# Attention results turned three units later, and attention products half a unit sooner, in a two-layer decoder trunk

## The chip, the cores and the metric

The kernel runs on one core of a Trainium2 chip. Its metric is the device time of one execution in microseconds, here the median of three runs. A profile is one further execution, recorded instruction by instruction; its times are counted from the first instruction. A core has a matrix engine (TensorE, PE in the profile, with its weight loads shown as PEld), three engines for elementwise work (VectorE or DVE, ScalarE or ACT, GpSimd or POOL) and SyncE (SP), whose queue here issues most of the transfers between memory and the core.

## The reference

The trunk has two layers of 256 tokens by 1024 features. Each layer is a SwiGLU block, a mixer and another SwiGLU block, each with a residual and a layer norm. The mixer projects its input to u, v, q, k, values and two gates; branch A gates u with a causal position mixing of v; branch B is differential attention with 8 heads. Cut to what matters here:

```python
def _diff_attention(q, k, v, lam):
    ...
        s = jnp.einsum('bqhmd,bkhmd->bhmqk', q_blk, k).astype(jnp.float32) * scale
        ...
        p = jax.nn.softmax(s, axis=-1)
        a = p[:, :, 0] - lam * p[:, :, 1]
        return jnp.einsum('bhqk,bkhe->bqhe', a.astype(v.dtype), v)

def _mixer(...):
    ...
    o = _diff_attention(q, k, val, lam_full)
    o = _rmsnorm(o, diff_ln_g) * (1.0 - lam_init)
    h_b = o.reshape(bsz, seq, DIFF_V_WIDTH)
    ...
    m = g[:, :, 0] * (h_a @ w_branch[0]) + g[:, :, 1] * (h_b @ w_branch[1])
    return m @ w_out
```

## The kernel before, in words

Every large product streams its float32 weights in chunks of 1 MB (128 x 2048 numbers). `stream` (L151) loads a chunk into one of four `raw` buffers through SyncE's queue, then ScalarE rounds it to a high part (`whi`, L170) and VectorE takes the low part by subtraction (`wlo`, L172). Products are then made of three matmuls: high by high, low by high, high by low (`three`, L239). `gemm_a2` (L244) makes output columns: it fills two PSUM banks of a chunk with 16 matmuls (L254), then adds the low parts with 16 shorter ones (L261), and ScalarE (L262) and VectorE (L264 or L266) empty the banks. `gemm_b` (L283) makes output rows, with `rows_b` (L273) doing six matmuls (L242) at a time. There are four "main" PSUM banks for these and four "side" banks for everything else.

TensorE's instructions keep the order in which the program is written (L59). The other engines' instructions are put in order by a planner that goes by its own estimates of when each is ready and, among ready ones, by their place in the program; each queue is then run in that order. `tc.issue_after`, wrapped as `behind(...)` (L147), ties an instruction behind a given earlier one on the same engine.

Small work is woven between the matmuls by a clock. After each piece of matmul work `beat(w)` (L124) advances it: 0.65 and 0.35 for the two parts of half a chunk in `gemm_a2`, 0.5 for six matmuls in `rows_b`, so that a 1 MB chunk's matmuls count 2. A task is a generator: `beside(task, delay)` starts it, and each `yield n` puts its next step at the first beat at or past n units after the step before. 

In the mixer the order of the matmuls is: values; for each of the four pairs of heads the projections to q and k (`rope`, L597, with a DMA that swaps the rotary halves, GpSimd's product L606 and VectorE's L605 and L610); then for each gate a chunk pair of rows and two chunks of columns (`gate_rows`, `gate_columns`); then two chunks of u, the rows of v, two more chunks of u; then the branch products, of which `branch_rows(1, hb)` is the first to read the attention's results `hb`.

The attention of a pair of heads is one task, `attend` (L616), started after its projections (L726: 4.5 units later, and 2.1 more for each further pair). Its steps are: scores into four side banks (L630); maxima and exponentials (L642, L644); the difference of the two softmaxes (L653); GpSimd parts the 16-bit halves of the numbers (`parted`, L182); SyncE issues DMA transposes of them (`moved`, L187); ScalarE joins the halves again (L678); TensorE multiplies with the values into a side bank (L684, L686); ScalarE copies the result out (L689) and takes squares in the same bank (L694); GpSimd makes reciprocal roots of the sums (`rsqrt4`, L224); ScalarE scales (L703); the result is parted, turned and joined in turn (L706, L708, L711, the last by VectorE, L193) and scaled into high and low parts of `hb` (L718, L720).

Of the kernel before, what the change touches and what calls it, by code (L numbers as in the profile page):

```python
# [54 lines left out]
def trunk(ctx, tc, x, xT, w13a, w13b, w2, wb, wqk, wu, wg, wgr, wbr, wbrr, wo, gateb, gatebr, sgug, sgub, sguwT, sgubias, lam, diffg,  # L55
# [25 lines left out]
    def side_bank():  # L81
        return psum.tile([P, 512], F32, tag="side", name=name("sbank"))
# [93 lines left out]
    def planes(v):  # L176
        return v.bitcast(U16).rearrange("p (w c) -> p w c", w=2)

    def numbers(v):
        return v.bitcast(U16).rearrange("p (c w) -> p w c", w=2)  # L180

    def parted(src, out):  # L182

        for w in range(2):
            G.tensor_copy(out=planes(out)[:, w], in_=numbers(src)[:, w])  # L185

    def moved(src, out):  # L187

        nc.sync.dma_start(out.bitcast(U16).rearrange("p (k t) -> p k t", t=P), src.bitcast(U16), transpose=True)
# [393 lines left out]
    def mixer(l, i, norm):  # L583
# [32 lines left out]
        def attend(hp, qT, kT):  # L616
# [58 lines left out]
            with behind(emptied[0]):  # L675
                for d, a in ((d1, aT1), (d0, aT0)):
                    for w in range(2):
                        A.activation(numbers(a)[:, w], planes(d)[:, w], AF.Copy)  # L678
            yield 2
            b = side_bank()  # L680
            for j in range(2):
                h = hp * 2 + j
# [21 lines left out]
            yield 0.4  # L704
            onT = slots("onT", 2)[0]
            parted(on, onT)  # L706
            yield 1.4
            moved(onT, on)  # L708
            yield 1.8
            with behind(added[0]):  # L710
# [12 lines left out]
        for hp in range(HEADS // 2):  # L723
            qT = rope(wqk[l, hp, 0], HD ** -0.5)
            kT = rope(wqk[l, hp, 1], 1.0)
            beside(attend(hp, qT, kT), 4.5 + 2.1 * hp)  # L726
            if hp == 1:
                gbias = bc_load(gatebr[l], qT[:, :1])
# [244 lines left out]
```

## Time and profile before

| | |
|---|---|
| median of 3 runs | 1229.89 us (1229.58 to 1230.67) |
| the profiled execution | 1231.39 us |
| its span, first to last instruction | 1229.7 us |
| TensorE busy | 1214.1 us, 99% of the span |
| VectorE, ScalarE, GpSimd busy | 886.2, 704.1 and 306.5 us |
| granted TensorE clock | 1.000 |
| mixers' stretches with attention | about 210 to 360 us (layer 0) and 817 to 968 us (layer 1) |
| TensorE waits of the products L684 | 5.6 us in 4 waits |
| TensorE waits of the scores L630 | 2.9 us in 4 waits |

Busy time is an average over a span in which the limits change, so a short wait on one engine is read from the timeline around it: what was the instruction waiting for, what stood behind it on the same engine, and who needed that. An instruction's row gives its start, its length and, in brackets, how long its engine had idled before it and whose end released it.

### The profile page before, as it was taken

The page shows a single profiled execution, that of the slowest core. Times are in us where ns is not written, and L with a number is a line of the kernel's source. Part 1 is how long each engine was busy: PE and PEld are TensorE (multiplying, and loading weights), DVE is VectorE, ACT ScalarE, POOL GpSimd, SP SyncE. Part 2 cuts the span into 40 slices and gives each one's busy share as a digit, 9 for nine tenths or more (in the row PEclk, how much of TensorE's full clock was granted, in tenths as well). Part 3 has the DMA queues.
Part 4 walks back from the last instruction along what each step waited for, and adds up shares of the span by engine and source line. Part 5 has one row for each costly group of instructions (what it writes and reads, how often), then busy time and mean ns, then how long its engine had stood idle before and what let it go on. Part 6 is the DMA issues. An engine that isn't in the chain of part 4 may idle for free.

```text
span 1229.7 us, 16740 instructions
## 1 busy us (share of the span) xinstructions
PE 1214.1 (99%) x5951; PEld 1020.0 (83%) x5951; DVE 886.2 (72%) x1498; ACT 704.1 (57%) x1338; POOL 306.5 (25%) x408
## 2 busy tenths in 40 slices
PE   9999999999999999999999999999999999999998
PEld 8888888888788888888888888888878888888887
DVE  6676767895689885766676766678856889676763
ACT  6475446667855655554455564466777555564740
POOL 1433100255431123230022330003453111333300
PEclk9999999999999999999999999999999999999999
DMA  8977645767766657767546857556657765667550
GB/s 342 301 222 233 238 176 191 247 209 200 212 205 202 212 163 227 248 197 257 201 158 210 249 178 259 200 207 213 222 147 233 225 204 211 171 228 252 176 183 35
DMA packets 108164, 259.63 MB, mean 211 GB/s; under 512 B 72576, under 2 KB 73648, under 8 KB 81968
## 3 DMA queue, kind: packets, MB, share of 16 engines
q1 hardware_dynamic: 103824, 244.87, 60.0%
q0 software_dynamic: 3824, 13.18, 3.6%
q8 instruction: 46, 0.75, 0.2%
q10 hardware_dynamic: 432, 0.52, 0.1%
q14 instruction: 38, 0.31, 0.1%
HBM read 236.52 MB, written 1.05 MB: 193 GB/s over the span
## 4 chain that ended last, share of the span: by engine, by line
PE 58%; DVE 7%; ACT 6%; DMA 3%; POOL 2%; issue 2%; SPq 0%; DVEq 0%; POOLq 0%; ACTq 0%
PE bank L242 48%; PE bank L254 6%; DVE wlo L172 3%; PE bank L261 2%; ACT whi L170 2%; DMA on<-onT 1%; ACT pp L644 1%; DMA swap<-z 1%; ACT aT L678 1%; PE sbank L804 1%; POOL swap L606 1%; ACT on L703 1%; DVE llo L172 1%; PE sbank L509 0%; DMA raw<-in_wu 0%
## 5 line engine op out<-in xcount | busy, mean ns | idle before, releaser
L172 DVE TENSOR_TENSOR wlo<-raw,whi 128x512 fp32r<-128x512 f32 (+1 forms) x570 | 524.3, 958 | 128.2 <-ACT whi L170 90.5
L170 ACT ACTIVATE whi<-raw 128x512 fp32r<-128x512 f32 (+1 forms) x570 | 432.6, 799 | 236.6 <-PE bank L242 177.1
L242 PE MATMUL bank<-whi,x 128*128 128x512 f32 x1480 | 462.6, 390 | 0.0
L242 PEld LDWEIGHTS bank<-whi,x 128*128 128x128 f32 x1480 | 277.9, 188 | 57.4
L242 PE MATMUL bank<-wlo,x 128*128 128x512 f32 x740 | 288.1, 389 | 0.0
L185 POOL COPY planes<-planes 128x512 uint16<-128x512 uint16 x80 | 86.4, 1108 | 318.2 <-DVE planes L541 318.2
L242 PEld LDWEIGHTS bank<-wlo,x 128*128 128x128 f32 x740 | 139.0, 188 | 28.2
L254 PE MATMUL bank<-x,whi 128*128 128x512 f32 x640 | 153.7, 392 | 0.2 <-DVE gz L264 0.2
L242 PE MATMUL bank<-whi,hhi 128*128 128x512 f32 (+1 forms) x374 | 141.2, 378 | 0.0
L242 PE MATMUL bank<-wlo,hhi 128*128 128x512 f32 (+1 forms) x374 | 141.0, 377 | 0.0
L242 PE MATMUL bank<-whi,hlo 128*128 128x512 f32 (+1 forms) x374 | 140.9, 377 | 0.0
L254 PEld LDWEIGHTS bank<-x,whi 128*128 128x128 f32 x640 | 118.0, 188 | 24.1 <-DVE gz L264 0.4
L193 POOL COPY planes<-planes 128x512 uint16<-128x512 uint16 x80 | 69.5, 913 | 94.0 <-DMA planes<-planes 93.7
L541 DVE TENSOR_TENSOR planes<-planes,bank 128x512 f32<-128x512 f32 x40 | 27.3, 682 | 87.5 <-issue 71.1
L606 POOL TENSOR_TENSOR swap<-swap,sin_t 128x512 f32<-128x512 f32 x16 | 28.3, 1770 | 231.4 <-DMA swap<-z 214.4
L261 PEld LDWEIGHTS bank<-x,wlo 128*128 128x128 f32 x640 | 81.4, 191 | 2.9
L540 ACT ACTIVATE planes<-bank 128x512 f32<-128x512 f32 x40 | 23.9, 598 | 104.4 <-PE bank L242 102.5
L261 PE MATMUL bank<-x,wlo 128*128 128x256 f32 x640 | 82.6, 283 | 0.0
L242 PEld LDWEIGHTS bank<-whi,hlo 128*128 128x128 f32 x374 | 70.4, 188 | 12.9
L242 PEld LDWEIGHTS bank<-whi,hhi 128*128 128x128 f32 x374 | 70.4, 188 | 12.8
L242 PEld LDWEIGHTS bank<-wlo,hhi 128*128 128x128 f32 x374 | 70.4, 188 | 12.8
L515 ACT ACTIVATE xf<-sbank,ln_b,ln_g 128x128 f32<-128x128 f32 x80 | 30.1, 457 | 41.2 <-PE sbank L509 41.2
(199 smaller groups left out, 1326.4 us busy)
## 6 DMA issues: line engine op xcount, KB each, us to landing
raw<-in_w13b SPq DMA_DIRECT2D x76, 1024.0 KB, 5.6
raw<-in_w SPq DMA_DIRECT2D x40, 1024.0 KB, 6.2
raw<-in_wb SPq DMA_DIRECT2D x16, 1024.0 KB, 5.0
raw<-in_wqk SPq DMA_DIRECT2D x16, 1024.0 KB, 4.9
raw<-in_w13a SPq DMA_DIRECT2D x8, 1024.0 KB, 5.1
raw<-in_wgr SPq DMA_DIRECT2D x8, 1024.0 KB, 5.2
raw<-in_wg SPq DMA_DIRECT2D x8, 1024.0 KB, 5.3
raw<-in_wu SPq DMA_DIRECT2D x8, 1024.0 KB, 6.1
```

Source lines behind the costliest of these rows:

```text
L170: A.activation(h, r, AF.Copy)
L172: V.tensor_tensor(out=w, in0=r, in1=h.bitcast(F32), op=ALU.subtract)
L185: G.tensor_copy(out=planes(out)[:, w], in_=numbers(src)[:, w])
L193: eng.tensor_copy(out=numbers(out)[:, w], in_=planes(src)[:, w])
L242: PE.matmul(ps, xx, w, start=start and n == 0, stop=stop and n == 2)
L254: PE.matmul(b[-1], hi[:, k * P : (k + 1) * P], xc(k), start=k == 0, stop=False)
L261: PE.matmul(b[n][:, :T], lo[:, k * P : (k + 1) * P], xc(k)[:, :T], start=False, stop=k == KT - 1)
L515: A.activation(xf[:, s], b[:, s], AF.Identity, scale=self.gT[:, f], bias=self.bT[:, f])
L540: silu[0] = A.activation(s, ps[0], AF.Silu).ins
L541: added[0] = V.tensor_tensor(out=s, in0=s, in1=ps[1], op=ALU.mult).ins
L606: turned_by[0] = G.tensor_tensor(out=s3, in0=s3, in1=s, op=ALU.mult).ins
L644: A.activation(p[:, s], p[:, s], AF.Exp, bias=mx[:, a], scale=-1.0, accum_out=sums[:, a])
```

## The change

Two numbers in `attend` change. The step with the products of attention weights and values comes 1.5 units after ScalarE's joining copies instead of 2. For the pairs of heads 0 and 1 the DMA transpose of the result comes 4.4 units after the parting copies instead of 1.4; pairs 2 and 3 keep 1.4. Steps that follow in the same task move with the step before them.

```diff
                 for d, a in ((d1, aT1), (d0, aT0)):
                     for w in range(2):
                         A.activation(numbers(a)[:, w], planes(d)[:, w], AF.Copy)
-            yield 2
+            yield 1.5
             b = side_bank()
             for j in range(2):
...
             yield 0.4
             onT = slots("onT", 2)[0]
             parted(on, onT)
-            yield 1.4
+            yield 4.4 if hp < 2 else 1.4
             moved(onT, on)
             yield 1.8
             with behind(added[0]):
                 joined(on, onT, V)
```

## The prediction

> **What bounds the kernel now.** I read the page's busy times first, then the stretches of the two mixers in which the attention runs beside the matmuls, then TensorE's waits, then each engine's timeline around those waits.
>
> The busy row is the page's first; the stretches show engine busy times (instructions in brackets) in the order PE, PEld, DVE, ACT, POOL.
>
> ```profile
> PE 1214.1 (99%) x5951; PEld 1020.0 (83%) x5951; DVE 886.2 (72%) x1498; ACT 704.1 (57%) x1338; POOL 306.5 (25%) x408
> ```
>
> ```profile
> 257.50:324.00 66.50, 64.15 (x358) 54.57 (x357) 46.72 (x111) 54.26 (x146) 33.26 (x57) 1.00 0.66 188
> 324.00:360.00 36.00, 34.45 (x174) 29.08 (x173) 24.63 (x46) 24.22 (x49) 14.93 (x34) 1.00 0.75 239
> ...
> 865.30:932.50 67.20, 63.92 (x358) 54.50 (x357) 47.77 (x114) 54.41 (x146) 32.87 (x57) 1.00 0.66 193
> 932.50:968.00 35.50, 33.96 (x170) 28.59 (x170) 23.59 (x43) 22.79 (x46) 14.78 (x34) 1.00 0.70 228
> ```
>
> TensorE is busy for all but 15.6 us of the span. The four stretches lose 2.35 + 1.55 + 3.28 + 1.54 = 8.7 us, and they are those in which the pairs of heads 0 to 3 go through their products. Of TensorE's own waits (total, times, longest) three rows lie there:
>
> ```profile
> PE sbank L684 <- ACT d L678: 5.6, 4, 1.5
> PE sbank L630 <- ACT sbank L694: 2.9, 4, 1.7
> ...
> PE bank L254 <- DVE gz L264: 0.2, 1, 0.2
> ```
>
> They add up to 5.6 + 2.9 + 0.2 = 8.7 us as well, so these three rows are the whole loss. L684 is the product of weights with values, which waits for ACT's copies L678; L630 are the scores, which need four PSUM side banks and wait for L694, the squares that are taken in the products' bank. Layer 0's TensorE timeline (start, length, instruction, and in brackets the idle time before it):
>
> ```profile
> 250.24 2.00 PE L254 MATMUL bank<-x,whi 128*128 128x512 f32 x8
> ...
> 268.45 0.38 PE L684 MATMUL sbank<-val,d 128*128 128x128 f32 x2
> ...
> 275.44 0.71 PE L630 MATMUL sbank<-qk,qk 64*128 64x128 f32 x6 [0.57 <-ACT sbank L694]
> ...
> 283.67 0.40 PE L242 MATMUL bank<-whi,x 128*128 128x512 f32 x1
> ...
> 289.14 0.38 PE L684 MATMUL sbank<-val,d 128*128 128x128 f32 x2
> ...
> 294.99 0.71 PE L630 MATMUL sbank<-qk,qk 64*128 64x128 f32 x6 [0.34 <-ACT sbank L694]
> ...
> 309.92 2.11 PE L254 MATMUL bank<-x,whi 128*128 128x512 f32 x8 [0.18 <-DVE gz L264]
> ...
> 313.29 0.46 PE L684 MATMUL sbank<-val,d 128*128 128x128 f32 x2 [1.26 <-ACT d L678]
> ...
> 332.56 0.46 PE L684 MATMUL sbank<-val,d 128*128 128x128 f32 x2 [1.55 <-ACT d L678]
> ```
>
> The L684 rows are the products of pairs 0, 1, 2 and 3. Pairs 0 and 1 wait for nothing; pair 2 waits 1.26 us and pair 3 1.55 us. The scores of pairs 2 and 3 wait 0.57 and 0.34 us. Layer 1 has the rest: 5.6 - 2.81 = 2.8 us at L684, and 2.9 - 0.91 = 2.0 us at L630, of which its longest wait is 1.7.
>
> Why is L678 late for pairs 2 and 3? The next fences are VectorE, ScalarE, GpSimd and SyncE of the same stretch.
>
> ```profile
> 289.33 0.69 DVE L738 TENSOR_TENSOR gr<-bank,bc 128x512 f32<-128x512 f32 x1 [2.29 <-PE bank L242]
> 297.46 0.80 DVE L193 COPY onT<-on 128x512 uint16<-128x512 uint16 x2 [7.43 <-DMA on<-onT]
> ...
> 310.91 0.42 DVE L264 TENSOR_TENSOR gz<-bank,r 128x256 f32<-128x256 f32 x1
> ```
>
> ```profile
> 263.58 0.81 ACT L678 ACTIVATE d<-d 128x256 uint16<-128x256 uint16 x2
> ...
> 285.56 0.82 ACT L678 ACTIVATE d<-d 128x256 uint16<-128x256 uint16 x2
> ...
> 300.87 0.51 ACT L644 ACTIVATE pp<-pp,mx 128x256 f32<-128x256 f32 x1 [5.94 <-DVE mx L642]
> ...
> 312.34 0.81 ACT L678 ACTIVATE d<-d 128x256 uint16<-128x256 uint16 x2
> ...
> 318.22 0.58 ACT L689 ACTIVATE on<-sbank 128x512 f32<-128x512 f32 x1
> ...
> 328.65 0.99 ACT L703 ACTIVATE on<-on,nwy 128x128 f32<-128x128 f32 x3 [1.70 <-POOL nwy L235]
> ...
> 331.62 0.79 ACT L678 ACTIVATE d<-d 128x256 uint16<-128x256 uint16 x2
> ```
>
> ```profile
> 246.85 1.63 POOL L185 COPY aT<-d 128x512 uint16<-128x512 uint16 x2
> ...
> 287.83 1.17 POOL L185 COPY onT<-on 128x512 uint16<-128x512 uint16 x2 [0.68 <-ACT on L703]
> ...
> 321.31 0.20 POOL L697 TENSOR_TENSOR ss<-s,ss 128x4 f32<-128x4 f32 x1 [7.82 <-ACT sbank L694]
> ...
> 327.50 1.13 POOL L235 TENSOR_TENSOR nwy<-nwa,nwy 128x4 f32<-128x4 f32 x1
> ```
>
> ```profile
> 248.51 1.25 SPq L189 DMA_TRANSPOSE d<-aT  x1
> ...
> 289.03 1.51 SPq L189 DMA_TRANSPOSE on<-onT  x1
> 290.63 4.92 SPq L189 DMA_TRANSPOSE d<-aT  x1
> ```
>
> VectorE stands still for 7.43 us, from 290.0 to 297.46, because L193 (the joining copy of pair 0's results, in `joined(on, onT, V)`) is next in its queue and the DMA transpose issued at 289.03 has not landed. Behind it stand the splits L172 and the maxima L642 of pair 3. ScalarE needs those maxima for its exponentials and idles 5.94 us until 300.87; L678 of pair 2 stands behind them and ends at 312.34 + 0.81 = 313.15, which is when TensorE goes on. From there the lateness is handed on: pair 2's copy L689 runs at 318.22 although its products started at 313.29, GpSimd's reciprocal roots run from 321.31 to 328.63 (its 7.82 us of idling are for L694), L703 waits 1.70 us for them, and L678 of pair 3, behind L703 in ScalarE's queue, ends at 332.41. Layer 1 repeats it:
>
> ```profile
> 905.95 0.84 DVE L193 COPY onT<-on 128x512 uint16<-128x512 uint16 x2 [7.06 <-POOL nwy L235]
> ```
>
> The row names a GpSimd instruction, but that was long done; the wait is again for the transpose.
>
> **The unit.** The program's clock runs in units that each stand for half of a 1 MB weight chunk's matmuls. Between 283.67 and 289.14 lie 24 matmuls of `rows_b`, two units: 2.74 us a unit, 1.37 us (six matmuls) for half of one. Count the clock from the first rope projection: projections to 16, gate rows 0 to 20, gate columns 0 to 24, gate rows 1 to 28, gate columns 1 to 32, u to 36, then v. A task goes on at the first beat at or past its due time.
>
> **Edit 1, `yield 2` to `yield 1.5` ahead of the products.** L678 of the pairs is issued at 18.0, 23.65, 30.65 and 36.5. So the products move from 20.0, 26.0, 32.65, 38.5 to 19.5, 25.5, 32.65 and 38.0: pair 2 does not move at all (32.15 still rounds up to 32.65), the others by six matmuls. Nothing is added or removed; 12 small matmuls change places with six large ones.
>
> Pairs 0 and 1 can afford it: L678 ended at 264.39 and 286.37, that is 4.06 and 2.77 us ahead of the products, against 1.37 needed. Cost nothing; if that cover were gone the price would be up to 1.37 us each. Pair 3 cannot, as things stand: its wait would become 1.55 + 1.37 = 2.92 us a layer. That is the price of edit 1 alone.
>
> What follows the products moves with them: the copy L689, the squares L694, GpSimd's 15 small operations, L703, the parting copies. For the scores' waits at L630 the squares come up to 1.37 us sooner. Of the four waits (0.57, 0.34, 1.7, and the remaining 0.3) three are smaller than that and one keeps 0.3: gain 2.9 - 0.3 = 2.6 us. Bounds: 0 (ScalarE's queue puts L689 no earlier) and 2.9.
>
> The later steps also pass the statements that they are tied to. L703 is held behind the latest emptying of a bank (`behind(emptied[0])`). Pair 0's goes from 24.0 to 23.3, and pair 1's from 29.65 to 29.3, in both cases to before the projection's first L262 of that half, so they may run as soon as GpSimd's roots are there.
>
> **Edit 2, `yield 1.4` to `yield 4.4` for pairs 0 and 1.** The transpose `moved(onT, on)` goes from 26.0 to 28.65 (pair 0) and from 32.65 to 34.65 (pair 1); `joined` from 28.0 to 30.65 and from 34.65 to 36.5; L718 and L720 from 28.65 to 31.3 and from 35.3 to 37.0. Per pair that is one DMA transpose on SyncE's queue, two DVE copies (0.80 us together), two ACT and two DVE operations.
>
> SyncE: in the program the transpose now stands behind pair 2's `d<-aT` (at 290.63 that one waited 4.92 us in issue behind it) and behind the weight loads of gate columns 1. But this queue goes by readiness: pair 0's `d<-aT` was issued at 248.51, the moment at which GpSimd's copies ended (246.85 + 1.63 = 248.48), 1.7 us ahead of its place in the program, clock 14.0, where the last projection's matmuls begin at 250.24. So I take it that the transpose still goes when GpSimd's parting copies end, as now (287.83 + 1.17 = 289.00, issued 289.03), if not sooner by edit 1. Bounds: issued at 289, or held until 28.65, about 300.
>
> VectorE: the copy is tied by `behind(added[0])`. At 28.0 that is the gate addition L738 of 289.33, and L193 stands right behind it. At 30.65 it is the addition L264 that ran at 310.91, and in an undelayed run some 5 us earlier. By then a transpose issued near 289 has landed (297.4), so the 7.43 us wait does not move: it is gone. What is late next? Pair 3's maxima are then limited by the scores themselves, which are done by 294.99 + 0.71 = 295.7, so ScalarE's exponentials start near 296 rather than at 300.87: about 5 us.
>
> Pair 2's products: L678 needs to come 1.26 us sooner and ScalarE's queue is 5 us ahead. Gain 1.26 and, for layer 1, about the same: 2.5 us. Bounds: 0 and 2.5.
>
> Pair 3's products: they are now due 1.37 us sooner, so 2.92 us are needed a layer. L689 of pair 2 can run right after its products (up to 5 us sooner than 318.22), and with it the roots, L703 and L678; TensorE itself is 1.4 us sooner there. So some 3.5 us of the 5 are left, which is only just enough. I keep 0.5 us of waiting a layer: gain 2 x (1.55 - 0.5) = 2.1 us. Bounds: -2.7 (no gain on ScalarE, the half unit in full) and +3.1.
>
> The 0.2 us at L254 go too. Pair 0's results now hold two activation tiles longer and come 2.65 units later into `hb`; the first matmul that reads `hb` is far away:
>
> ```profile
> L242 PE MATMUL bank<-whi,hb x64: 389/389/476, 360.1 to 980.2; 128*128 128x512 f32 x64
> ```
>
> Pair 1's L720 at 37.0 is near 330, some 30 us ahead of it; cost nothing.
>
> The planner orders four engines anew, which can bring a wait that is not in this trace: for that I take two of the size that L684 shows (1.26 to 1.55), each half as likely as not, 1.4 us in all. Bounds: 0 and one such in each layer, 2.9.
>
> Sum: -2.6 - 2.5 - 2.1 - 0.2 + 1.4 = **-6.0 us**. Later stages are TensorE's, so the gain reaches the end whole. The profiled execution took 1231.39 us (span 1229.7), 1.5 more than the median of the runs, 1229.89; 1231.4 - 6.0 = 1225.4 in its terms, 1223.9 in the median's.
>
> **A rule beside the rows.** How long the transposes fly decides how much of edit 2 would remain if the queue did hold them back.
>
> ```profile
> DMA to landing us min/median/max: 3.0/7.0/8.3
> ```
>
> ```profile
> raw<-in_wb SPq DMA_DIRECT2D x16, 1024.0 KB, 5.0
> ```
>
> The results' transposes (128 x 512 float32, 256 KB) take 7.0 us in the middle and 8.3 at most, longer than a plain load of four times the bytes. The Trainium skill (Advanced Engine Details and Errata, X-Bar Transpose (TRN2)) says that transposes are as fast as regular DMAs, and its DMA: Bandwidth & Descriptors (Latency and other measured facts) gives 261 GB/s, an estimate of 1.0 us for these bytes; the trace disagrees. By the pages' rate a held-back transpose would land well inside the two units before `joined`, and rival A below would give the forecast's time; by the row it does not.
>
> **Rivals.** A, *held back*: the transpose is issued at 28.65, near 300, lands 8.3 us later and meets L193 at 30.65, near 305: VectorE waits about 3 us in the gate columns. TensorE has four main banks, two for each 1 MB chunk, so it can run one chunk (two units, 5.5 us) ahead and feels little; the lateness handed to pair 3 stays. For: the place in the program is all that the edit changes. Against: the issue at 248.51. Gain 2.6 + 2.5 + 0.2 - 1.4 = 3.9, less pair 3's half unit when half felt (1.4): -2.5 to -4, 1226.6 as its middle.
>
> B, *no difference*: the half unit's debt at pair 3 (+2.7) eats what the scores gain (-2.6), and ScalarE's L678 of pair 2 finds another instruction ahead of it. For: L678 stands behind L703, which needs GpSimd's chain, not VectorE. Against: pair 2's L678 had no such wait, only the 5.94. Within 2.5 us of 1229.9.
>
> C, *slower*: VectorE's wait moves instead of going. L193 is placed behind L264 of the first gate column chunk with the transpose not landed, for the 7.43 us seen now; the L264 of the second chunk stands behind it, then L750 and L678 on ScalarE, so pair 2 waits as before. It decides once the wait exceeds the 5.5 us that the main banks cover: 7.43 - 5.5 = 1.9 us a layer at L254, plus pair 3's 1.37: 2 x 3.3 = 6.6, less 2.6 at the scores: +4.0, 1233.9. Against it: the transpose would have to be issued after 300.
>
> **How the numbers follow.** Forecast 0.56, own range -8.7 to -3 (all of the loss gone; or pair 3 not gained): 1221.2 to 1226.9. A 0.18, B 0.14, C 0.12. About 0.2%, 2.5 us, is what a measurement of this kernel tells from no change. Faster: forecast and A, 0.74; the same: B, 0.14; slower: C, 0.12. The range takes the full loss with 0.7 us for the runs' spread as its low end, 1220.5, and reaches up through A and the nearer half of B, 1230.5.
>
> **What would show it.** In the changed profile the products should lie six matmuls sooner for pairs 0, 1 and 3 and stay for pair 2; VectorE's wait at L193 of pair 0 should be gone and L193 stand behind an L264; ScalarE's wait for L642 should fall from 5.94 to under 1.5 us; L684 should wait under 1.5 us in all instead of 5.6, and L630 under 0.6 instead of 2.9. The transposes of pair 0 should still be issued when GpSimd's copies end. It is wrong if L193 still waits for its DMA, if pair 3's products wait more than 1.5 us a layer, or if a new TensorE wait over 1.5 us stands in these stretches.

## The result

The changed kernel takes 1221.72 us (1221.21 to 1222.89) where the kernel before, on the same chip, takes 1230.04: a ratio of 0.9933, 95% interval 0.9916 to 0.9951, or 8.3 us less. Measured once more beside the second group of experiments it gave 1220.37 us, ratio 0.9914 (0.9900 to 0.9927). The profiled execution took 1221.21 us, its span 1219.2 us against 1229.7.

The page's busy times and the four stretches in which the products lie (same columns and same times as before, so not exactly the same matmuls):

```profile
PE 1210.7 (99%) x5951; PEld 1018.1 (84%) x5951; DVE 890.4 (73%) x1498; ACT 708.2 (58%) x1338; POOL 302.5 (25%) x408
```

```profile
257.50:324.00 66.50, 66.50 (x374) 57.09 (x373) 51.40 (x109) 59.25 (x153) 36.32 (x67) 1.00 0.69 220
324.00:360.00 36.00, 35.73 (x179) 30.13 (x178) 28.15 (x54) 23.32 (x44) 9.99 (x24) 1.00 0.59 195
...
865.30:932.50 67.20, 65.35 (x373) 55.91 (x372) 49.79 (x101) 58.67 (x144) 36.07 (x66) 1.00 0.71 221
932.50:968.00 35.50, 35.50 (x173) 29.99 (x173) 30.03 (x56) 21.29 (x39) 8.29 (x23) 1.00 0.62 204
```

TensorE's idle time in these stretches fell from 8.7 to 0 + 0.27 + 1.85 + 0 = 2.1 us. Of the three rows of waits one is left; the scores' L630 and the bank wait L254 are gone:

```profile
PE sbank L684 <- ACT d L678: 2.1, 3, 1.4
```

Layer 0's timeline, and layer 1's two remaining waits:

```profile
266.32 0.38 PE L684 MATMUL sbank<-val,d 128*128 128x128 f32 x2
...
285.96 0.38 PE L684 MATMUL sbank<-val,d 128*128 128x128 f32 x2
...
308.81 0.38 PE L684 MATMUL sbank<-val,d 128*128 128x128 f32 x2
...
325.35 0.46 PE L684 MATMUL sbank<-val,d 128*128 128x128 f32 x2 [0.27 <-ACT d L678]
```

```profile
889.19 0.46 PE L684 MATMUL sbank<-val,d 128*128 128x128 f32 x2 [0.49 <-ACT d L678]
...
929.76 0.46 PE L684 MATMUL sbank<-val,d 128*128 128x128 f32 x2 [1.37 <-ACT d L678]
```

Pairs 0, 1 and 2 of layer 0 wait for nothing, pair 3 for 0.27 us; in layer 1 pair 1 waits 0.49 us, which is new, and pair 3 1.37. VectorE, ScalarE, GpSimd and SyncE around them:

```profile
303.21 0.74 DVE L264 TENSOR_TENSOR gz<-bank,r 128x256 f32<-128x256 f32 x2
303.87 1.34 DVE L193 COPY onT<-on 128x512 uint16<-128x512 uint16 x2
```

```profile
281.19 0.39 ACT L703 ACTIVATE on<-on,nwy 128x128 f32<-128x128 f32 x1
...
283.64 1.42 ACT L678 ACTIVATE aT<-d 128x512 uint16<-128x512 uint16 x2
...
294.30 0.51 ACT L644 ACTIVATE pp<-pp,mx 128x256 f32<-128x256 f32 x1 [1.64 <-DVE mx L642]
...
305.12 0.81 ACT L678 ACTIVATE d<-d 128x256 uint16<-128x256 uint16 x2
```

```profile
282.00 1.18 POOL L185 COPY onT<-on 128x512 uint16<-128x512 uint16 x2
```

```profile
283.21 1.33 SPq L189 DMA_TRANSPOSE on<-onT  x1
...
287.48 1.23 SPq L189 DMA_TRANSPOSE d<-aT  x1
```

The join L193 of pair 0 no longer idles VectorE: it stands behind the L264 additions at 303.21, and its transpose was issued at 283.21. ScalarE's wait for pair 3's maxima is 1.64 us instead of 5.94, pair 2's L678 ends at 305.93 instead of 313.15, and the lateness that was handed from pair to pair is not there to hand on. One thing is earlier than the prediction had it: the last L703 of pair 0 ends at 281.58, ahead of pair 1's L678. In the kernel before it ran behind that L678 (which ended at 286.38), right after the last L262 of gate columns 0, the emptying of a bank to which it was tied:

```profile
286.23 0.36 ACT L262 ACTIVATE r<-bank 128x256 f32<-128x256 f32 x1
286.48 1.28 ACT L703 ACTIVATE on<-on,nwy 128x128 f32<-128x128 f32 x4
```

GpSimd's parting copies begin at 282.00 instead of 287.83, and the transpose leaves 5.8 us sooner. That proved to be the larger part of the story.

Two of the prediction's signs were missed narrowly: L684 waits 2.1 us in all where under 1.5 was asked, and ScalarE's wait for the maxima is 1.64 us where under 1.5 was asked. None of the signs of being wrong appeared: pair 0's join waits in neither layer.

### The profile page after: what moved, and what is told of

Read it like the earlier page. It is cut to its first block, busy times and chain, and to the rows that moved or that the text cites. A ratio compares the mean times of both kernels' runs of the same rounds, so it can differ in the third digit from the quotient of the medians.

```text
span 1219.2 us, 16735 instructions
## 1 busy us (share of the span) xinstructions
PE 1210.7 (99%) x5951; PEld 1018.1 (84%) x5951; DVE 890.4 (73%) x1498; ACT 708.2 (58%) x1338; POOL 302.5 (25%) x408
## 5 line engine op out<-in xcount | busy, mean ns | idle before, releaser
L254 PE MATMUL bank<-x,whi 128*128 128x512 f32 x640 | 153.3, 391 | 0.0
L254 PEld LDWEIGHTS bank<-x,whi 128*128 128x128 f32 x640 | 118.2, 188 | 23.8
L193 POOL COPY planes<-planes 128x512 uint16<-128x512 uint16 x80 | 70.6, 926 | 92.2 <-DMA planes<-planes 92.0
```

The costliest lines, as they stand in the source:

```text
L193: eng.tensor_copy(out=numbers(out)[:, w], in_=planes(src)[:, w])
L254: PE.matmul(b[-1], hi[:, k * P : (k + 1) * P], xc(k), start=k == 0, stop=False)
```

## The experiments

Each is given as a diff against the kernel before, unless it says otherwise. Theory and rivals changed after the first group, so the groups are told in order. Each group had runs of the kernel before beside it, which took 1230.05 us for the first four kernels, 1231.13 us for the two that take the first edit apart, the first of the candidates and the repeated changed kernel, and 1230.58 us for the join alone and the last two candidates; gains and ratios are against these.

**The first edit alone.**

```diff
-            yield 2
+            yield 1.5
             b = side_bank()
```

> Only the first edit: the products half a unit sooner, every transpose at 1.4 as before. Theory J (the cost is VectorE's join L193 standing ahead of pair 3's maxima while its transpose flies; both edits work on it): the join keeps its place right behind the gate addition L738, but the transpose of pair 0 is issued some 5 us sooner (near 283 instead of 289), since L703 no longer stands behind pair 1's L262; it lands near 290, and the join waits 1 to 2 us instead of 7.4. Then most of the gain is there without the second edit: 1223 to 1226 us, L630 near 0, L684 2 to 4 us. Rival P (my priced sum: edit 1 gains 2.6 at the scores and pays 1.37 a layer at pair 3, and only edit 2 frees VectorE): 1229 to 1231 us, L193 still waiting 6 us or more, L684 7 to 8 us.

Measured: 1220.77 us (1219.37 to 1221.83), ratio 0.9920 (0.9906 to 0.9933). TensorE's one wait in the mixers, then VectorE and SyncE:

```profile
PE sbank L684 <- ACT d L678: 1.0, 1, 1.0
```

```profile
289.33 0.69 DVE L738 TENSOR_TENSOR gr<-bank,bc 128x512 f32<-128x512 f32 x1 [2.12 <-PE bank L242]
289.94 0.81 DVE L193 COPY onT<-on 128x512 uint16<-128x512 uint16 x2
```

```profile
283.67 1.23 SPq L189 DMA_TRANSPOSE on<-onT  x1
```

The join stands where it stood in the kernel before, right behind L738, and runs at once: the transpose left at 283.67 and has landed. The first edit alone has the whole gain, so my priced sum for it (2.6 gained, 2.7 paid) is wrong. Theory J was too cautious: it expected 1223 us or more and 1 to 2 us of waiting at the join. The one wait of 1.0 us is that of pair 1 in layer 1 (at 890.00), not of pair 3.

**The second edit alone.**

```diff
-            yield 1.4
+            yield 4.4 if hp < 2 else 1.4
             moved(onT, on)
```

> Only the second edit: products at 2 as before, pairs 0 and 1 turned at 4.4. Theory J and the priced sum agree that the join of pair 0 now stands behind an L264 of gate columns 1, so its 7.4 us wait is gone, pair 2's products wait for nothing and pair 3's little, while the scores keep their L630 waits of 2.9 us: 1224 to 1226 us. Rival H (the gain is the half unit's, through the scores and the side banks): 1228 to 1230 us, L684 still above 4 us.

Measured: 1222.59 us (1222.46 to 1225.12), ratio 0.9939 (0.9927 to 0.9952).

```profile
PE sbank L630 <- ACT sbank L694: 1.7, 4, 0.7
```

```profile
289.93 1.23 SPq L189 DMA_TRANSPOSE d<-aT  x1
291.27 4.34 SPq L189 DMA_TRANSPOSE on<-onT  x1
```

```profile
306.74 0.79 DVE L193 COPY onT<-on 128x512 uint16<-128x512 uint16 x2
```

L684 does not wait at all, not even pair 3; what is left is the scores' wait, 1.7 us. Here pair 0's transpose goes late, at 291.27 and behind pair 2's, and the join goes later still. GpSimd's copies for it had ended at 287.63 + 1.17 = 288.80, so its place behind pair 2's, whose own copies ended at 289.90, held it back by 2.5 us; layer 1 shows the same 2.5. The time lies below the 1224 to 1226 us that were expected. So either edit alone takes away nearly everything, and together they take away no more: they are two ways to the same 7.4 us, not two terms of a sum.

**The transpose at its old place, the join three units later** (with the first edit).

```diff
-            yield 2
+            yield 1.5
...
             moved(onT, on)
-            yield 1.8
+            yield 4.8 if hp < 2 else 1.8
```

> Both edits, but the three units stand after the transpose instead of ahead of it: the transpose keeps its old place in the program (1.4), only the join and what follows come three units later (4.8 after it instead of 1.8). Theory J: the transpose is issued when its data are ready in either case, so this is the changed kernel again, 1221 to 1223 us, with the transposes of pair 0 issued at the same time within 1 us. Rival Q (the transpose's place in SyncE's queue, behind pair 2's transposes and the loads, is what helps): nearer the first edit alone, 1224 us or more.

Measured: 1220.59 us (1220.08 to 1221.02), ratio 0.9918 (0.9905 to 0.9932).

```profile
283.65 1.23 SPq L189 DMA_TRANSPOSE on<-onT  x1
...
287.92 1.23 SPq L189 DMA_TRANSPOSE d<-aT  x1
```

The transpose is issued 0.4 us from where the changed kernel issues it, and SyncE's order is the same: with the first edit in, its place in the program does not matter. Since the first edit alone turned out as fast, the time does not tell theory from rival here; the queue's times do.

**Pair 3's products back at 2** (against the changed kernel).

```diff
-            yield 1.5
+            yield 1.5 if hp < 3 else 2
```

> The changed kernel with pair 3's products back at 2 units (pairs 0 to 2 at 1.5). Theory: what is left at L684 in the changed kernel is 0.27 and 1.37 us at pair 3 and 0.49 at pair 1 of layer 1; with pair 3 six matmuls later its waits go, and nothing that matters waits for pair 3's results: 1.5 us faster than the changed kernel, near 1220.2 us, L684 at 0.5. Rival (the later products push pair 3's own chain into the first reader of hb, or the plan is reordered): no gain, 1221.5 or more.

Measured: 1218.98 us (1218.69 to 1219.35), ratio 0.9905 (0.9892 to 0.9919), with 0.3 us left at L684:

```profile
PE sbank L684 <- ACT d L678: 0.3, 1, 0.3
```

This is on the theory's side, and lower than its 1220.2 us. The 0.3 us are pair 1's in layer 0. It is the lowest time so far, though its interval overlaps that of the changed kernel's second measurement.

**What in the first edit does it?** It moves the products, and with them all that follows in the task. L703 of pair 0 is due at 23.3 instead of 24.0 and so is tied behind an earlier emptying of a bank: the last two L262 of gate columns 0 come after it (the expectations call the one it was tied to pair 1's). The next two kernels take these apart.

L703 ahead of that statement, the products at their old place:

```diff
             r = rsqrt4(ss, 1.0 / (2 * HD))
-            yield 2.6
+            yield 2 if hp < 2 else 2.6
```

> The kernel before with one number changed for pairs 0 and 1: 2.0 instead of 2.6 units ahead of L703, products and transposes at their old numbers. L703 of pair 0 then stands ahead of pair 1's L262 (23.3 instead of 24.0), while the products stay at 20.0. Theory X (the transposes' early start, through L703's place in ScalarE's queue, is what removes the lateness): pair 0's transpose goes before 287 instead of 289.03, the join waits 4 us or less, L684 falls under 2.5 us, L630 stays near 2.9: 1223 to 1226 us. Rival S (the products' half unit, through the squares and the side banks, is the cause): 1229 to 1231 us.

Measured: 1221.29 us (1220.90 to 1222.19), ratio 0.9921 (0.9908 to 0.9935).

```profile
281.42 0.99 ACT L703 ACTIVATE on<-on,nwy 128x128 f32<-128x128 f32 x3 [0.25 <-POOL nwy L235]
...
283.12 0.39 ACT L703 ACTIVATE on<-on,nwy 128x128 f32<-128x128 f32 x1
...
285.57 1.40 ACT L678 ACTIVATE aT<-d 128x512 uint16<-128x512 uint16 x2
```

```profile
285.13 1.38 SPq L189 DMA_TRANSPOSE on<-onT  x1
```

```profile
289.78 0.79 DVE L193 COPY onT<-on 128x512 uint16<-128x512 uint16 x2
```

```profile
PE sbank L630 <- ACT sbank L694: 2.0, 2, 1.0
```

No product is moved, yet nearly all of the gain is there, 9.8 us against the kernel before beside it (1223 to 1226 us had been expected). The 2.0 us that the half unit takes from the scores remain.

The products half a unit sooner, L703 back at its old place:

```diff
-            yield 2
+            yield 1.5
             b = side_bank()
...
-            yield 2.6
+            yield (3.3, 3.1, 2.6, 2.6)[hp]
```

> The other half: products at 1.5 as in the change, the second edit left out, and L703 of pairs 0 and 1 put back at its old place (24.0 and 29.65) by 3.3 and 3.1 units ahead of it. Theory X: the transpose of pair 0 goes near 288 again, the join waits 6 us or more, L630's waits are gone, but L684 is 6 us or more, since pair 3's products stand half a unit sooner: 1228 to 1231 us, which is what my priced sum had for the first edit alone. Rival S: 1220 to 1223 us as for the first edit alone.

Measured: 1233.18 us (1229.91 to 1236.83), ratio 1.0015 (1.0003 to 1.0027).

```profile
PE sbank L684 <- ACT d L678: 8.2, 4, 2.9
...
PE bank L254 <- DVE gz L264: 1.8, 2, 1.4
```

```profile
284.41 1.27 ACT L703 ACTIVATE on<-on,nwy 128x128 f32<-128x128 f32 x4
```

```profile
286.94 1.67 SPq L189 DMA_TRANSPOSE on<-onT  x1
288.70 5.09 SPq L189 DMA_TRANSPOSE d<-aT  x1
```

```profile
295.10 0.81 DVE L193 COPY onT<-on 128x512 uint16<-128x512 uint16 x2 [5.51 <-DMA on<-onT]
```

```profile
330.17 0.77 PE L684 MATMUL sbank<-val,d 128*128 128x128 f32 x2 [2.89 <-ACT d L678]
```

No gain, rather a little loss. The transpose goes at 286.94, the join waits 5.51 us (6 or more was expected), pair 2 waits as before, and pair 3 waits 2.89 us: the 1.55 + 1.37 = 2.92 that the prediction had priced for the first edit if nothing else moved. The time came out above the 1231 that was expected, with 1.8 us at L254 that were not foreseen. The loss itself is mostly the clock's: in the profiled execution the granted clock of TensorE fell to 0.50 towards the end of that wait, at about 329.5, and came back at about 336.3; the mean clocks of the 11 runs are 0.994 to 0.999, those of the kernel before beside them 0.999 or 1.000. The first product's row above is 0.77 us long instead of 0.46. From the first rope projection to the position mixing layer 0 takes 162.7 us, 2.6 more than in the kernel before; layer 1, with a wait of 2.88 us at pair 3 but no fall of the clock, takes 160.7 against 160.8. So the half unit by itself is worth nothing here; what it carried across was.

**The join alone.** Is it VectorE's standing at the join that costs, or pair 2's transpose, which is held in SyncE's issue behind pair 0's? Everything as before, the join of pairs 0 and 1 alone, with what follows it, three units later:

```diff
             moved(onT, on)
-            yield 1.8
+            yield 4.8 if hp < 2 else 1.8
```

> The kernel before with the join of pairs 0 and 1 alone three units later (1.4 then 4.8 instead of 1.8): products, L703, the transposes and SyncE's order are as before, pair 0's transpose ahead of pair 2's. Theory J (what costs is VectorE standing at the join; how the transpose comes to be landed by then does not matter): pair 0's transpose still goes near 289 and pair 2's behind it is still held in issue for some 5 us, yet L193 waits 1 us or less, pair 2's products wait for nothing: 1221.5 to 1224 us, as the second edit alone (1222.6). Rival T (pair 2's transpose, late behind pair 0's, is what makes L678 late, and the earlier start of pair 0's is what helps): 1228 us or more, L684 above 4 us.

Measured: 1223.25 us (1221.65 to 1224.00), ratio 0.9936 (0.9923 to 0.9949).

```profile
288.28 1.34 SPq L189 DMA_TRANSPOSE on<-onT  x1
289.71 5.99 SPq L189 DMA_TRANSPOSE d<-aT  x1
```

```profile
306.19 0.79 DVE L193 COPY onT<-on 128x512 uint16<-128x512 uint16 x2
```

```profile
PE sbank L630 <- ACT sbank L694: 1.9, 4, 0.8
```

Pair 0's transpose goes at 288.28 as before, pair 2's is held 5.99 us behind it, longer than before, and still L684 is free and 7.3 us are gained. So it is VectorE's wait that costs; a change of SyncE's order is not needed.

**For the fastest.** Three candidates with pair 3's products at 2 (no profile with them there shows a wait of pair 3): the first edit for pairs 0 to 2 alone, then with the join three units later, then the changed kernel so amended a second time.

```diff
-            yield 2
+            yield 1.5 if hp < 3 else 2
```

> Candidate for the fastest: the first edit for pairs 0 to 2 alone, pair 3's products at 2, the second edit left out. Theory: the first edit alone (1220.8) without pair 3's wait (1.0 us shown at L684): 1219 to 1220 us, about as fast as the changed kernel with pair 3 at 2 (1219.0). Rival (the second edit is worth something once pair 3 is out of the way): over 1220 us.

Measured: 1220.53 us (1219.32 to 1220.94), ratio 0.9912 (0.9899 to 0.9926). Not 1219 to 1220; within what can be told the same as the changed kernel beside it. The expectation laid the first edit's 1.0 us to pair 3; it was pair 1's, so moving pair 3 had nothing to take away. Here 0.6 us remain at L684, at pair 1 of layer 0.

> The changed kernel itself, unaltered, beside the next runs on the same chip: 1221.7 us as before, within 1 us. If it comes out near 1220.7, the first edit alone and the changed kernel are the same within what can be told.

Measured: 1220.37 us (1220.02 to 1221.18).

```diff
-            yield 2
+            yield 1.5 if hp < 3 else 2
...
-            yield 1.8
+            yield 4.8 if hp < 2 else 1.8
```

> Candidate for the fastest: products at 1.5 for pairs 0 to 2 and at 2 for pair 3, transposes at 1.4, the join of pairs 0 and 1 three units later. All three TensorE waits should be gone (L684 under 0.5, L630 and L254 at 0): 1218.5 to 1220 us. Rival: the changed kernel has nothing left to gain there, the same as the changed kernel on this chip within 0.5 us.

Measured: 1219.77 us (1219.13 to 1220.20), ratio 0.9909 (0.9896 to 0.9923); 0.8 us remain at L684, again at pair 1 of layer 0, where under 0.5 had been expected.

> The changed kernel with pair 3's products at 2, once more, beside the candidate above: 1219.0 us was measured, 1.4 to 2.7 below the changed kernel. Theory: again about 1 us below it (1219 to 1220). Rival: it was the spread between chips, 1220.4 or more.

Measured: 1219.04 us (1218.98 to 1220.34), ratio 0.9907 (0.9893 to 0.9921), with no L684, L630 or L254 wait in its profile. Twice 1219.0, so this is the lowest time found; but its interval overlaps that of the changed kernel, and the three candidates are not told apart.

## Why the prediction was right or wrong

**The time.** Forecast 1223.9, measured 1221.7, the forecast's side and inside its own range of 1221.2 to 1226.9. That the total came near is in part luck: the sum has the removal of the 7.43 us wait once, under edit 2, and the changed kernel has two cures for it. The rows of waits were summed well: 6.0 us of net gain were expected and the wait rows fell by 8.7 - 2.1 = 6.6. The stretches between the same matmuls of both profiles, from the first rope projection to the first product of the position mixing (before, then after; the first column pair is TensorE's busy time), show more:

```profile
209.57:369.60 160.03, 156.13 (x859) 133.35 (x858) 122.01 (x243) 110.82 (x250) 62.98 (x101) 1.00 0.69 218
...
817.34:978.10 160.76, 155.94 (x859) 133.35 (x858) 121.99 (x241) 110.71 (x250) 61.79 (x101) 1.00 0.68 216
```

```profile
208.80:363.76 154.96, 154.69 (x859) 132.72 (x858) 125.71 (x243) 112.50 (x250) 60.49 (x101) 1.00 0.69 228
...
811.39:968.14 156.75, 154.90 (x859) 132.74 (x858) 126.19 (x243) 112.54 (x250) 60.47 (x101) 1.00 0.69 226
```

They are 5.07 and 4.01 us shorter, 9.1 in all. Idle time accounts for 3.90 + 4.82 - 0.27 - 1.85 = 6.6 of it, and TensorE's busy time over the same 859 matmuls for 1.44 + 1.04 = 2.5. So a part of the waiting had stood in the rows as busy matmuls; my sum took the rows for the whole. The scores of pair 3 in layer 0, before and after, up to the next matmul:

```profile
293.30 1.35 PE L630 MATMUL sbank<-qk,qk 64*128 64x256 f32 x10
...
295.62 0.50 PE L242 MATMUL bank<-whi,x 128*128 128x512 f32 x1
```

```profile
291.50 1.58 PE L630 MATMUL sbank<-qk,qk 64*128 64x256 f32 x16
293.00 0.50 PE L242 MATMUL bank<-whi,x 128*128 128x512 f32 x1
```

From start to start that is 2.32 us with the wait and 1.50 without: the wait cost 0.82 us where its row says 0.34. The other three waits of the scores fall short by the same 0.47 to 0.49 us, 1.9 in all. A wait at L684 falls short by less, 0.24 us at pair 3 of layer 0 (against the kernel with pair 3 at 2). So the term that was most mis-sized is the scores': 2.6 us in the sum, 2.9 + 1.9 = 4.8 measured. The expectations of the first edit alone, the second alone, pair 3 back at 2 and L703 alone were too high as well, by 1.2 to 2.2 us. The Trainium skill (Perfetto Trace Analysis, Tensor Engine Instruction (MATMUL, LD_WEIGHTS)) says that TensorE's end times are estimated rather than observed, and the rows agree: matmuls that start 0.23 us apart (24 in 5.47 us) are drawn 0.39 us long, and so hide the first 0.16 us of a wait behind the last of them. Where the rest of the 0.48 us at the scores is hidden stays open. The rest of the 10.5 us between the two spans lies in the first 30 us and the last 6, where the change does nothing; the medians differ by 8.3.

**Edit 1: the step that failed.** The prediction gave it 2.6 us at the scores against 2.7 at pair 3, in all nothing, and left the 7.4 us to edit 2. Alone it measured -9.3 us (1220.77 against 1230.05). The cause was written down and not followed: L703 of pair 0 "may run as soon as GpSimd's roots are there", and the transpose goes "if not sooner by edit 1". The parting copies behind L703 began sooner, the transpose left 5.4 us sooner (283.67 against 289.03), and the join, in its old place behind L738, found it landed. The experiment with L703 alone (1221.3) and the one without it (1233.2) show that this crossing of one statement carries the edit. What was priced, the half unit itself, was priced rightly by the rows: pair 3's 2.92 came as 2.89 when L703 stayed behind, and the scores' 2.6 came as 2.9, all of it gone.

**Edit 2.** Right in mechanism: the join ties itself to a later addition, the 7.43 us wait goes, pair 2 is free. It is sufficient (1222.6 alone, 1223.3 with only the join and what follows it moved) but in this change it is not needed, since edit 1 has already taken the same wait. The sum knew this one cure only, and took edit 1 for a term beside it.

**SyncE by readiness.** Right for the changed kernel: the transpose that stands three units later in the program was issued when its copies ended (282.00 + 1.18 = 283.18, issued 283.21). Rival A, held back, did not come up here. As a rule it does not hold: in the second edit alone the same place in the program put the transpose behind pair 2's and held it back by 2.5 us after its copies. The join three units later found it landed even so, at 306.74, so no run shows the 3 us of VectorE's waiting that A was priced at.

**Pairs 0 and 1 "cost nothing".** Wrong for pair 1 by a little: the changed kernel's profile has 0.49 us at its products in layer 1, another profile of it 0.71 us in layer 0, and the other kernels with its products at 1.5 and L703 ahead have 0.28 to 1.01 us there, but for one with none. L703 now stands ahead of pair 1's L678 on ScalarE (281.19 and 283.64 above), which together with the half unit's 1.37 us uses up the cover of 2.77 us. This is about the new wait for which 1.4 us were taken.

**Pair 3.** Half a microsecond a layer was kept; the profile shows 0.27 and 1.37. With its products at 2 the wait is gone and the time 1 us or so lower; that the one makes the other is not shown, since the changed kernel's second profile has no wait at pair 3 at all and that execution still took 1220.02 us.

**Rivals B and C.** B's condition, L678 of pair 2 behind something else, did not arise. C, a wait that moves into the gate columns, did not either; the kernel with L703 held back shows how the slower side looks (L684 8.2 us, L254 1.8), but by another way than C's, since there the wait had never gone.

**The time of the transposes in flight.** The changed kernel's landings of the results' transposes

```profile
DMA to landing us min/median/max: 2.8/4.0/7.6
```

are shorter than before (median 4.0 instead of 7.0 us), still far from the estimate of 1.0 us by the rate of the Trainium skill (DMA: Bandwidth & Descriptors, Latency and other measured facts). That rate bears on rival A alone, which did not come up.

## What to carry to other kernels

When an engine's queue runs in a fixed order, find the one instruction at which it stands for a transfer; both starting the transfer sooner and queueing that instruction later cure it, and one cure is enough. Before pricing a half step, follow every later statement of the moved task and ask which instruction each is newly tied behind: here one such crossing alone was worth nearly 10 us and the half step alone nothing. And compare starts with starts: TensorE's short waits cost 0.24 to 0.49 us more than their rows say in this case.

## What was not expected of the hardware

A DMA transpose that SyncE issues soon after another one of 256 KB is held in issue: 4.92 us in the kernel before (1.6 us after it), 4.34 and 5.99 us in the second edit alone and in the join alone (1.3 and 1.4 us after). The kept profiles have 16 such places, in four kernels, 1.3 to 2.2 us after the other transpose, and each was held, for 3.8 to 6.0 us. With another, half as large, transpose and a weight load between, 4.3 us after it, the same issue took 1.23 us; and the half as large one itself went out 2.2 us after one of 256 KB in 1.19 us. Whether the distance, the size or the queue in between decides was not tried.

A wait of TensorE of 2.89 us was followed by 6.8 us at half the granted clock (0.50) in the profile with L703 held back, and a wait of 2.88 us in its other layer was not. No other profile shows so long a wait in the mixers. Why the one and not the other stays open.
